# A hybrid decoder layer on one core: half of K in the gate and up projections by seven block products, two of the four weight sums by adding DMAs

## The chip, the cores and the metric

The kernel runs on one core of a Trainium2 chip. The metric is the device time of one execution in microseconds (us); the time given for a kernel is the median of several executions. The engines of the core are PE (matmuls; its weight loads are PEld), DVE and ACT (elementwise work), POOL and SP (here they mainly issue DMAs). Each engine takes its instructions in the order in which the program gives them to it, and waits on semaphores for the others.

## The reference, cut to what matters

One layer over 256 tokens of width 2048, in float32, then a last norm. The mixer (three kinds of attention, gates, output projection) is not touched by the change; the SwiGLU part is.

```python
D_MODEL, SEQ, D_FF = 2048, 256, 5632

def rms_norm(x, g):
    y = x * rsqrt(mean(x * x, axis=-1, keepdims=True) + 1e-6)
    return y * g

def swiglu(h, w_gate, w_up, w_down):
    return (silu(h @ w_gate) * (h @ w_up)) @ w_down

x = x + hybrid_mixer(rms_norm(x, norm_mix_g), ...)
x = x + swiglu(rms_norm(x, norm_ffn_g), w_gate, w_up, w_down)
return rms_norm(x, final_norm_g)
```

## The kernel before, in words

**Matmuls.** All large products go through one scheme. The activations stand transposed (K on the partitions), 128 tokens of them are the loaded operand of a matmul, and 512 columns of a weight are what moves through. To keep float32 accuracy with the faster number format fp32r, each operand is split into a high part (rounded to fp32r) and a low part (the rest), and three products are summed in one PSUM bank: activation high x weight high (L714), high x weight low (L715), low x weight high (L716). In the trace `wh`/`wl` are the parts of a weight, `hq` holds the parts of h, `th`/`tl` those of another transposed operand, `acc` is the bank.

**Pieces.** A weight comes in pieces of 512 rows of K by 512 columns, 1 MB each, loaded by SP (L630) into one of 3 `raw` buffers. A piece is split in two halves of 256 rows: ACT copies the high part (L655) and DVE subtracts it from the raw weights for the low part (L656), 1024 elements per partition each. There are 4 buffers for parts, and `split` runs 3 halves ahead of the products (`AHEAD`). A half feeds 12 matmuls: 2 k-tiles of 128 rows, 2 halves of the tokens (128 each), 3 products.

**Jobs.** A job is one output of 256 tokens by 512 columns: its list of pieces and a closing function. The main loop (L718) goes through the jobs in a fixed order: the mixer's, then four for the output projection (`evac_out`, which makes h, transposed and split, in four quarters of K, keys `("h2", c)`), then for each of 11 blocks j a gate job and an up job, then four of the down projection with 11 pieces each. Per half the loop calls `split` for the half that lies 3 ahead, then `advance(1)`, which lets one step of the waiting side work (a queue of generators, `side`) into the program, then the 12 matmuls.

**Gate and up.** `evac_fg` applies Silu to the two banks of a gate job (ACT, L540); `evac_fu` multiplies with the up banks (DVE, L548) and queues `to_quad`: two groups of four transposes on PE (L203), each followed by the split of 512 elements on ACT (L212) and DVE (L213). The result stays in SBUF until the down jobs read it. A block is 2 jobs x 8 halves x 12 = 192 matmuls.

## Time and profile before

| | |
|---|---|
| time, median of 3 runs | 1689.5 us (1688.86 to 1689.72) |
| the profiled execution: its time / its span | 1689.31 us / 1687.6 us |
| mean granted clock of PE | 0.999 |
| busy: PE, DVE, ACT, POOL | 1675.3, 928.4, 757.0, 28.4 us |
| matmul and transpose instructions on PE | 7644 |
| HBM traffic | 188 GB/s over the span |

The span is the time from the first to the last instruction in the trace; the execution's own time has a little more around it. Busy time is summed per engine; PE's weight loads overlap its matmuls. The granted clock is the share of TensorE's full clock that the chip allowed, 1.00 being 2.4 GHz.

### The profile page before, as it was taken

The numbers are of one execution on the slowest core, as the hardware profiler recorded it, in microseconds if no ns is written. First come the engines' busy times: TensorE is split into PE (matmuls) and PEld (weight loads), VectorE is DVE, ScalarE is ACT, GpSimd is POOL, SyncE is SP. The second block draws the span as 40 slices with busy tenths as digits, with TensorE's granted clock in tenths as the row PEclk, the third lists the DMA queues.
The fourth block names the chain that finished last, engine by engine and source line by source line (L and its number), as shares of the span: only waits on it lengthen the run. The fifth ranks groups of instructions, "written<-read, shape, count | busy, mean of one in ns | idle before, by whom it ended". The sixth has DMA issues, their size and how long they took to land.

```text
span 1687.6 us, 19009 instructions
## 1 busy us (share of the span) xinstructions
PE 1675.3 (99%) x7644; PEld 1380.5 (82%) x7644; DVE 928.4 (55%) x1074; ACT 757.0 (45%) x943; POOL 28.4 (2%) x43
## 2 busy tenths in 40 slices
PE   9999999999999999999999999999999999999997
PEld 6878788888888888888888888888888888888886
DVE  6676765656565656555565555444454445554454
ACT  6354544445444444444445544444444444444443
POOL 2100000000000000000000000000000000000000
PEclk9999999999999999999999999999999999999999
DMA  8545455455555655655655555555555556555553
GB/s 282 188 157 175 150 175 175 157 176 179 181 186 197 204 196 191 206 204 197 222 190 184 178 197 185 189 198 179 197 188 186 197 180 221 182 193 198 197 186 116
DMA packets 47321, 318.06 MB, mean 188 GB/s; under 512 B 5552, under 2 KB 5824, under 8 KB 10240
## 3 DMA queue, kind: packets, MB, share of 16 engines
q1 hardware_dynamic: 44640, 309.35, 52.7%
q0 software_dynamic: 1872, 6.43, 1.5%
q8 instruction: 60, 0.98, 0.2%
q10 hardware_dynamic: 720, 1.06, 0.2%
q14 instruction: 29, 0.24, 0.0%
HBM read 314.72 MB, written 2.10 MB: 188 GB/s over the span
## 4 chain that ended last, share of the span: by engine, by line
PE 99%; DMA 1%; ACT 0%; DVE 0%; SPq 0%; issue 0%; ACTq 0%
PE acc L714 32%; PE acc L716 31%; PE acc L715 31%; PE tps L203 2%; PE sps L242 1%; DMA raw<-w_in_t 1%; PE sps L255 0%; PE sps L256 0%; PE sps L254 0%; PE sps L293 0%; PE sps L294 0%; PE sps L295 0%; SPq L177 0%; ACT x L605 0%; SPq L628 0%; DVE wl L656 0%
## 5 line engine op out<-in xcount | busy, mean ns | idle before, releaser
L656 DVE TENSOR_TENSOR wl<-raw,wh 128x1024 fp32r<-128x1024 f32 x580 | 713.1, 1231 | 714.9 <-ACT wh L655 714.7
L655 ACT ACTIVATE wh<-raw 128x1024 fp32r<-128x1024 f32 x580 | 614.4, 1060 | 820.8 <-PE acc L716 798.1
L714 PE MATMUL acc<-wh,hq 128*128 128x512 f32 x1664 | 663.5, 399 | 0.1
L715 PE MATMUL acc<-wl,hq 128*128 128x512 f32 x1664 | 648.1, 390 | 1.7 <-DVE wl L653 1.0
L716 PE MATMUL acc<-wh,hq 128*128 128x512 f32 x1664 | 649.5, 390 | 0.0
L716 PEld LDWEIGHTS acc<-wh,hq 128*128 128x128 f32 x1664 | 312.3, 188 | 67.4
L715 PEld LDWEIGHTS acc<-wl,hq 128*128 128x128 f32 x1664 | 313.1, 188 | 65.0 <-DVE wl L653 2.2
L714 PEld LDWEIGHTS acc<-wh,hq 128*128 128x128 f32 x1664 | 312.7, 188 | 64.5 <-issue 2.7
L714 PE MATMUL acc<-wh,th 128*128 128x512 f32 x472 | 184.6, 391 | 0.0
L716 PE MATMUL acc<-wh,tl 128*128 128x512 f32 x472 | 183.8, 389 | 0.0
L715 PE MATMUL acc<-wl,th 128*128 128x512 f32 x472 | 183.6, 389 | 0.0
L716 PEld LDWEIGHTS acc<-wh,tl 128*128 128x128 f32 x472 | 88.6, 188 | 18.5
L715 PEld LDWEIGHTS acc<-wl,th 128*128 128x128 f32 x472 | 88.6, 188 | 18.1
L714 PEld LDWEIGHTS acc<-wh,th 128*128 128x128 f32 x472 | 88.6, 188 | 18.2
L714 PE MATMUL acc<-wh,oh 128*128 128x512 f32 x192 | 74.7, 389 | 0.0
L715 PE MATMUL acc<-wl,oh 128*128 128x512 f32 x192 | 74.7, 389 | 0.0
L716 PE MATMUL acc<-wh,ol 128*128 128x512 f32 x192 | 74.7, 389 | 0.0
L716 PEld LDWEIGHTS acc<-wh,ol 128*128 128x128 f32 x192 | 36.0, 188 | 7.5
L715 PEld LDWEIGHTS acc<-wl,oh 128*128 128x128 f32 x192 | 36.0, 188 | 7.5
L714 PEld LDWEIGHTS acc<-wh,oh 128*128 128x128 f32 x192 | 36.0, 188 | 7.5
L266 ACT ACTIVATE sc<-sc,mx 128x128 f32<-128x128 f32 (+1 forms) x32 | 14.3, 448 | 20.2 <-DVE mx L264 19.3
L213 DVE TENSOR_TENSOR tl<-tps,th 128x512 fp32r<-128x512 f32 x30 | 20.5, 684 | 0.0
(161 smaller groups left out, 602.9 us busy)
## 6 DMA issues: line engine op xcount, KB each, us to landing
raw<-w_in_t SPq DMA_DIRECT2D x116, 1024.0 KB, 4.8
raw<-w_fg_t SPq DMA_DIRECT2D x44, 1024.0 KB, 4.8
raw<-w_fu_t SPq DMA_DIRECT2D x44, 1024.0 KB, 4.9
raw<-w_fd_t SPq DMA_DIRECT2D x44, 1024.0 KB, 4.8
raw<-w_branch_t SPq DMA_DIRECT2D x24, 1024.0 KB, 4.8
raw<-w_out_t SPq DMA_DIRECT2D x16, 1024.0 KB, 4.8
raw<-w_in_t SPq DMA_DIRECT2D x7, 512.0 KB, 8.7
bias<-b_gate_r POOLq DMA_DIRECT2D x12, 256.0 KB, 4.2
```

Source lines behind the costliest of these rows:

```text
L203: nc.tensor.transpose(dst[:, i * P:(i + 1) * P], s, ident)
L213: nc.vector.tensor_tensor(l, ps, h.bitcast(F32), OP.subtract)
L242: nc.tensor.matmul(ps[:, a:b], qt[lo:hi, h, t * P:(t + 1) * P], kt[lo:hi, h, 0:b - a], start=True, stop=True)
L266: nc.scalar.activation(sc[:, a:b], sc[:, a:b], AF.Exp, bias=mx[:, t:t + 1], accum_out=sums[:, t:t + 1])
L655: nc.scalar.activation(h, r, AF.Copy)
L656: nc.vector.tensor_tensor(l, r, h.bitcast(F32), OP.subtract)
L714: nc.tensor.matmul(acc, a, wh[:, i], start=pi == 0 and k == 0, stop=False)
L715: nc.tensor.matmul(acc, a, wl[:, i], start=False, stop=False)
L716: nc.tensor.matmul(acc, b, wh[:, i], start=False, stop=pi == npieces - 1 and k == 3)
```

## The change

Only the gate and up projections, their result's way to the down projection, and the pools of buffers change.

The K of 2048 is cut in four quarters of 512. For quarters 0 and 1 the product of the 256 tokens (two halves t of 128) with the up and gate columns of block j is taken as a product of 2 x 2 blocks: A(t, k) times B(k, n), n = 0 for up and n = 1 for gate; B11, B12, B21, B22 are up and gate of quarter 0, up and gate of quarter 1, each a piece of 512 x 512. Instead of eight block products, seven are made (Strassen's scheme in Winograd's form), from sums on both sides. Quarters 2 and 3 are computed as before, two token halves by two columns each.

- The left operands (four sums of A's blocks, and the seven splits) are made once by `combine`, in the steps after the second job of the output projection.
- The four sums of weights are made for each block: B11 += B12 and later B11 += B22 by DVE, in place in the raw buffer; B12 += B22 and the last B11 += B21 by a DMA on POOL's queue that adds the piece from HBM into the raw buffer (`accum_op`).
- `ffn_job` lays out 11 units per block, numbered 0 to 10 in the order of its last lines: an `m_unit` is one block product of 12 matmuls on a single bank, a `p_unit` a plain piece of 24 matmuls on two banks. A unit's `prep` makes sums and splits the whole piece (`whole`, 2048 elements per partition, in place of two halves), its `emit` the matmuls, and then `after`, if it has one.
- There are four banks, b1, b5, b6, b8. `keep` copies a bank to SBUF on ACT when it must be used for another sum: m1 (behind unit 0), m5 (behind unit 2), u2 (behind unit 4), u3 (behind unit 6). Behind u3 the gate's Silu is taken; `last`, behind unit 10, closes the up columns with three DVE operations.
- Parts and raw pieces now share one pool of 12 buffers (`big`): in this stage 6 raw pieces and 3 split units. `prepare_units` calls `prep` of unit u+2 ahead of unit u's matmuls, as many as there are buffers.
- The result f of a block is transposed, copied on ACT and written to DRAM (`f_out`); the first job of the down projection loads it back (`f_load`) and splits it (`f_split`).

A block has 7 x 12 + 4 x 24 = 180 matmuls. The core of the diff:

```diff
 NEG = -1e37
 
-RAW_BUFS = 3
-SPLIT_BUFS = 4
-AHEAD = 3
-SLOTS = 27
+BIGS = 12
+SLOTS = 25
+RAWS = {"mix": 3, "ffn": 6, "down": 3}
+PARTS = {"mix": 4, "ffn": 6, "down": 4}
 LAST = 6
...
+    ht = {}
+
+    def combine(key, h1, h2):
+
+
+        a = {(t, q): h[:, :, t * P:(t + 1) * P] for t in range(2) for q, h in enumerate((h1, h2))}
+        t12 = slot([P, 2, 4, P], "s12")
+        t34 = slot([P, 2, 4, P], "s34")
+        s1, s2, s3, s4 = t12[:, 0], t12[:, 1], t34[:, 0], t34[:, 1]
+        nc.vector.tensor_tensor(s1, a[1, 0], a[1, 1], OP.subtract)
+        nc.vector.tensor_tensor(s2, s1, a[0, 0], OP.subtract)
+        nc.vector.tensor_tensor(s3, a[0, 0], a[1, 0], OP.subtract)
+        nc.vector.tensor_tensor(s4, a[0, 1], s2, OP.add)
+        yield
+        ops = []
+        for v in (a[0, 0], a[0, 1], s4, a[1, 1], s1, s2, s3):
+            p = slot([P, 2, 4, P], "sp", F32R)
+            nc.scalar.activation(p[:, 0], v, AF.Copy)
+            nc.vector.tensor_tensor(p[:, 1], v, p[:, 0].bitcast(F32), OP.subtract)
+            ops.append((p[:, 0], p[:, 1]))
+            yield
+        quads[key] = ops
+        yield
+
...
+                if c < 2:
+                    ht[c] = slot([P, 4, S], "ht")
+                else:
...
+                        if c < 2:
+                            nc.scalar.activation(ht[c][:, k], pk, AF.Copy, scale=gk)
+                            continue
...
+                if c == 1:
+                    yield from combine(("s", 0), ht[0], ht[1])
...
-        job([(w_fu[j, kp], ("h2", kp)) for kp in range(4)], evac_fu(j))
+    f_t = [scratch.tile([P, 4, S], F32, name=f"f_t{j}") for j in range(NCF)]
+
+    def f_out(j, f):
+
+        yield
+        ft = slot([P, 4, S], "ft")
+        for t in range(2):
+            ps = tps()
+            transposes(ps, [f[:, t, i * P:(i + 1) * P] for i in range(4)])
+            nc.scalar.activation(ft[:, :, t * P:(t + 1) * P], ps.rearrange("p (a b) -> p a b", a=4), AF.Copy)
+            if t == 1:
+                nc.gpsimd.dma_start(f_t[j], ft)
+            yield
+
+    f_in = {}
+
+    def f_load(q):
+        if q < NCF:
+            f_in[q] = slot([P, 4, S], "fin")
+            nc.gpsimd.dma_start(f_in[q], f_t[q])
+
+    def f_split(q):
+        h, l = new_both() if q < 4 else new_quad("f")
+        src = f_in.pop(q)
+        nc.scalar.activation(h, src, AF.Copy)
+        nc.vector.tensor_tensor(l, src, h.bitcast(F32), OP.subtract)
+        quads["f", q] = (h, l)
+
+    def ffn_job(j):
+
+
+
+
+
+        B = {(k, n): (j, k, n) for k in range(4) for n in range(2)}
+        B11, B12, B21, B22 = B[0, 0], B[0, 1], B[1, 0], B[1, 1]
+        aps = {(j, k, n): (w_fu, w_fg)[n][j, k] for k in range(4) for n in range(2)}
+        for key in (B22, B11, B12, B[2, 1], B[3, 1], B21, B[2, 0], B[3, 0]):
+            want(key, aps[key], "ffn")
+        bank = {}
+        v = {}
+
+        def add(dst, src):
+            nc.vector.tensor_tensor(raw[dst], raw[dst], raw[src], OP.add)
+
+        def m_unit(op, key, name, adds=(), drop=(), after=None, then=None):
+            def prep():
+                for d, s in adds:
+                    add(d, s)
+                w = whole(raw[key])
+                if then:
+                    nc.gpsimd.dma_start(raw[then[0]], aps[then[1]], accum_op=OP.add)
+                release(*drop)
+                return w
+
+            def emit(w):
+                first = name not in bank
+                if first:
+                    bank[name] = accp.tile([P, 512], F32, tag="acc", name="acc")
+                sh, sl = quad(("s", 0))[op]
+                three(bank[name], sh, sl, w, first, True, True)
+                if after:
+                    after()
+            units.append((2, "ffn", prep, emit))
+
+        def p_unit(k, n, after=None):
+            def prep():
+                w = whole(raw[B[k, n]])
+                release(B[k, n])
+                return w
+
+            def emit(w):
+                qh, ql = quad(("h2", k))
+                for t, name in enumerate((("b1", "b6"), ("b5", "b8"))[n]):
+                    first = name not in bank
+                    if first:
+                        bank[name] = accp.tile([P, 512], F32, tag="acc", name="acc")
+                    three(bank[name], qh[:, :, t * P:(t + 1) * P], ql[:, :, t * P:(t + 1) * P], w, first, True,
+                          True)
+                if after:
+                    after()
+            units.append((2, "ffn", prep, emit))
+
+        def keep(name, b):
+            def f():
+                if name == "m1":
+                    v["m"] = slot([P, 2, 512], "m")
+                    v["u"] = slot([P, 2, 512], "u")
+                v[name] = v["m" if name[0] == "m" else "u"][:, int(name in ("m5", "u3"))]
+                nc.scalar.activation(v[name], bank[b], AF.Copy)
+                if name == "u2":
+                    nc.vector.tensor_tensor(v["m5"], v["m5"], v["u2"], OP.subtract)
+                if name == "u3":
+                    quad("rs2")
+                    s = v["s"] = slot([P, 2, 512], "sg")
+                    nc.vector.tensor_tensor(s[:, 0], bank["b5"], v["m5"], OP.add)
+                    nc.vector.tensor_tensor(s[:, 1], bank["b8"], v["u3"], OP.subtract)
+                    for t in range(2):
+                        nc.scalar.activation(s[:, t], s[:, t], AF.Silu, scale=rs2[:, t:t + 1])
+            return f
+
+        def last():
+
+            s = v["s"]
+            nc.vector.tensor_tensor(s[:, 1], bank["b6"], s[:, 1], OP.mult)
+            nc.vector.tensor_tensor(v["m1"], bank["b1"], v["m1"], OP.add)
+            nc.vector.tensor_tensor(s[:, 0], v["m1"], s[:, 0], OP.mult)
+            side.append(f_out(j, s))
+
+        m_unit(2, B22, "b5")
+        m_unit(0, B11, "b6", after=keep("m1", "b6"))
+        m_unit(4, B11, "b8", adds=[(B11, B12)], after=keep("m5", "b8"), then=(B12, B22))
+        p_unit(2, 1)
+        m_unit(5, B11, "b6", adds=[(B11, B22)], drop=[B22], after=keep("u2", "b6"), then=(B11, B21))
+        p_unit(3, 1)
+        m_unit(6, B12, "b6", drop=[B12], after=keep("u3", "b6"))
+        m_unit(1, B21, "b1", drop=[B21])
+        p_unit(2, 0, after=(lambda: (f_load(0), f_load(1))) if j == NCF - 1 else None)
+        m_unit(3, B11, "b6", drop=[B11])
+        p_unit(3, 0, after=last)
...
+    def release(*keys):
+        for k in keys:
+            del raw[k]
+        pump()
+
+    def three(acc, ah, al, w, start, stop, again=False):
+
+        wh, wl = w
+        n = wh.shape[1]
+        skip = again and not start
+        for k in range(n):
+            nc.tensor.matmul(acc, ah[:, k], wh[:, k], start=start and k == 0, stop=False, skip_group_check=skip)
+            nc.tensor.matmul(acc, ah[:, k], wl[:, k], start=False, stop=False, skip_group_check=skip)
+            nc.tensor.matmul(acc, al[:, k], wh[:, k], start=False, stop=stop and k == n - 1,
+                             skip_group_check=skip)
+
+    def whole(r):
+        h = big([P, 4, 512], "wh", F32R)
+        l = big([P, 4, 512], "wl", F32R)
+        nc.scalar.activation(h, r, AF.Copy)
+        nc.vector.tensor_tensor(l, r, h.bitcast(F32), OP.subtract)
+        return h, l
...
+    pump()
+    ready = deque()
+    held = 0
+    at = 0
+
+    def prepare_units(n):
+
+        nonlocal at, held
+        while at < len(units) and at < n:
+            need, stage, prep, _ = units[at]
+            if held + need > PARTS[stage]:
+                break
+            ready.append(prep())
+            held += need
+            at += 1
+
+    prepare_units(3)
...
+    for u, (need, stage, _, emit) in enumerate(units):
+        prepare_units(u + 4 if stage == "mix" else len(units))
+        advance(1)
+        emit(ready.popleft())
+        held -= need
```

The first place that matters is DVE's order around the beginning of a block (tile numbers are those of the program). Before, at the seam from block 3 to block 4 (the others read alike), DVE had splits (L656), the two multiplications of `evac_fu` (L548) and the splits of the transposed result (L213):

```order
L656 TENSOR_TENSOR wl_8247<-raw_8164,wh_8246 128x1024
L548 TENSOR_TENSOR sg_8121<-acc0_8124,sg_8121 128x512
L548 TENSOR_TENSOR sg_8121<-acc1_8125,sg_8121 128x512
L656 TENSOR_TENSOR wl_8267<-raw_8164,wh_8266 128x1024
L656 TENSOR_TENSOR wl_8285<-raw_8198,wh_8284 128x1024
L213 TENSOR_TENSOR tl_8289<-tps_8290,th_8288 128x4x128
L656 TENSOR_TENSOR wl_8310<-raw_8198,wh_8309 128x1024
L213 TENSOR_TENSOR tl_8289<-tps_8315,th_8288 128x4x128
```

After the change DVE has at the beginning of block 6 the low part of unit 1 (L784, wl_8418), the three operations of `last` (L670 to L672), the sum B11 += B12 (L609), the low parts of units 2 and 3, the sum B11 += B22, and the low part of unit 4:

```order
L784 TENSOR_TENSOR wl_8418<-raw_8282,wh_8417 128x2048
L670 TENSOR_TENSOR sg_8347<-acc_8203,sg_8347 128x512
L671 TENSOR_TENSOR m_8216<-acc_8358,m_8216 128x512
L672 TENSOR_TENSOR sg_8347<-m_8216,sg_8347 128x512
L609 TENSOR_TENSOR raw_8282<-raw_8282,raw_8302 128x2048
L784 TENSOR_TENSOR wl_8450<-raw_8282,wh_8449 128x2048
L784 TENSOR_TENSOR wl_8468<-raw_8332,wh_8467 128x2048
L609 TENSOR_TENSOR raw_8282<-raw_8282,raw_8252 128x2048
L784 TENSOR_TENSOR wl_8498<-raw_8282,wh_8497 128x2048
```

The sums now stand in the queue ahead of the low parts that read them, and the first one behind the closing operations of the block before.

On ACT the same place had, before, high parts of halves (L655) with the high parts of the transposed result (L212) between them:

```order
L655 ACTIVATE wh_8246<-raw_8164 128x1024
L655 ACTIVATE wh_8266<-raw_8164 128x1024
L655 ACTIVATE wh_8284<-raw_8198 128x1024
L212 ACTIVATE th_8288<-tps_8290 128x4x128
L655 ACTIVATE wh_8309<-raw_8198 128x1024
L212 ACTIVATE th_8288<-tps_8315 128x4x128
L655 ACTIVATE wh_8334<-raw_8232 128x1024
```

After the change ACT has the high parts of units 2 (wh_8449) and 3 (wh_8467), the first copy of the old block's transposes (L575), the copy of bank b6 as m1 (L655, acc_8480), the high part of unit 4 (wh_8497), the second copy of the transposes, and the copy of bank b8 as m5 (acc_8511):

```order
L783 ACTIVATE wh_8449<-raw_8282 128x2048
L783 ACTIVATE wh_8467<-raw_8332 128x2048
L575 ACTIVATE ft_8473<-tps_8474 128x4x128
L655 ACTIVATE m_8493<-acc_8480 128x512
L783 ACTIVATE wh_8497<-raw_8282 128x2048
L575 ACTIVATE ft_8473<-tps_8504 128x4x128
L655 ACTIVATE m_8493<-acc_8511 128x512
L783 ACTIVATE wh_8525<-raw_8356 128x2048
```

The copy that frees b8 for unit 3's second half thus stands behind the split of unit 4.

## Rows read from the trace of the kernel before

**Rows 1.** The page: span, busy totals, and the chain that ended last by engine.

```profile
span 1687.6 us, 19009 instructions
...
PE 1675.3 (99%) x7644; PEld 1380.5 (82%) x7644; DVE 928.4 (55%) x1074; ACT 757.0 (45%) x943; POOL 28.4 (2%) x43
...
PE 99%; DMA 1%; ACT 0%; DVE 0%; SPq 0%; issue 0%; ACTq 0%
```

**Rows 2.** Busy time (us) in a stretch of the gate/up stage.

```profile
core 0: us, PE busy (x) PEld busy (x) DVE busy (x) ACT busy (x) POOL busy (x), PEclk, DMA share, GB/s
993.00:1037.50 44.50, 44.50 (x202) 36.85 (x201) 22.04 (x22) 19.21 (x20) 0.00 (x0) 1.00 0.55 189
```

**Rows 3.** Timeline of PE: start, duration, engine, line, operation, tiles, shape, count.

```profile
992.63 0.39 PE L714 MATMUL acc<-wh,hq 128*128 128x512 f32 x1
...
995.35 0.39 PE L714 MATMUL acc<-wh,hq 128*128 128x512 f32 x1
995.58 0.39 PE L715 MATMUL acc<-wl,hq 128*128 128x512 f32 x1
...
996.04 0.60 PE L203 MATMUL tps<-ident,sg 128*128 128x128 f32 x4
...
996.70 0.40 PE L715 MATMUL acc<-wl,hq 128*128 128x512 f32 x1
```

**Rows 4.** Chain that ended last (start, us, what): two neighbouring blocks' transposes.

```profile
1396.46 0.44 PE tps L203 x4
...
1440.93 0.44 PE tps L203 x4
```

**Rows 5.** Timeline of ACT and DVE; in brackets the idle time before and its releaser.

```profile
1396.49 1.06 ACT L655 ACTIVATE wh<-raw 128x1024 fp32r<-128x1024 f32 x1 [1.66 <-PE acc L716]
...
1397.46 0.58 ACT L212 ACTIVATE th<-tps 128x512 fp32r<-128x512 f32 x1
1397.59 1.23 DVE L656 TENSOR_TENSOR wl<-raw,wh 128x1024 fp32r<-128x1024 f32 x1 [1.50 <-ACT wh L655]
```

**Rows 6.** Timeline, a matmul and the split that it releases.

```profile
899.98 0.39 PE L716 MATMUL acc<-wh,tl 128*128 128x512 f32 x1
...
900.41 1.06 ACT L655 ACTIVATE wh<-raw 128x1024 fp32r<-128x1024 f32 x1 [1.60 <-PE acc L716]
```

**Rows 7.** Groups of instructions by line and shape: count, busy us, mean ns.

```profile
L655 ACT ACTIVATE wh<-raw 128x1024 fp32r<-128x1024 f32 x580 | 614.4, 1060 | 820.8 <-PE acc L716 798.1 <-issue 12.5 <-ACT sig L434 7.7
...
L212 ACT ACTIVATE th<-tps 128x512 fp32r<-128x512 f32 x30 | 17.4, 581 | 0.0
...
L540 ACT ACTIVATE sg<-acc,rs 128x512 f32<-128x512 f32 x22 | 15.1, 690 | 9.7 <-PE acc L716 9.7
L548 DVE TENSOR_TENSOR sg<-acc,sg 128x512 f32<-128x512 f32 x22 | 14.1, 682 | 0.0
...
L458 DVE TENSOR_TENSOR sig<-sig,sig 128x1024 f32<-128x1024 f32 x8 | 9.8, 1225 | 0.3
...
L401 ACT ACTIVATE k<-acc 128x512 f32<-128x512 f32 x12 | 7.2, 599 | 7.4 <-PE acc L716 7.4
...
L582 DVE TENSOR_TENSOR x<-x,gfin 128x512 f32<-128x512 f32 x6 | 4.0, 690 | 0.3
...
L652 ACT ACTIVATE wh<-raw 128x512 fp32r<-128x512 f32 x4 | 2.4, 627 | 3.4 <-DMA raw<-w_in_t 3.4
```

**Rows 8.** DMA issues: queue, count, KB of each, median us to landing.

```profile
raw<-w_fg_t SPq DMA_DIRECT2D x44, 1024.0 KB, 4.8
...
gfin<-gfin_r POOLq DMA_DIRECT2D x1, 1024.0 KB, 5.0
```

**Rows 9.** Busy time by stretch, the end of the span (columns as in rows 2).

```profile
1678.00:1679.00 1.00, 0.52 (x3) 0.09 (x1) 0.44 (x2) 0.00 (x0) 0.00 (x0) 1.00 0.00 0
1681.00:1682.00 1.00, 0.00 (x0) 0.00 (x0) 0.86 (x5) 0.20 (x1) 0.00 (x0) 1.00 0.00 0
...
1683.00:1684.00 1.00, 0.00 (x0) 0.00 (x0) 0.00 (x0) 0.67 (x1) 0.00 (x0) 0.50 0.84 313
```

More of the change, by code (lines that the diff above doesn't have):

```diff
@@ L67, in slot, with big @@
         return slots.tile(shape, dt, tag="slot", name=name)
+    def big(shape, name, dt=F32):
+        return bigs.tile(shape, dt, tag="big", name=name)
     def sm(shape, name):
@@ L165, in new_both @@
     def new_both():
[L167 to L168 removed]
+        t = big([P, 2, 4, S], "hq", F32R)
+        return t[:, 0], t[:, 1]
     xq = {}
@@ L552, in trunk @@
-    for j in range(NCF):
-        job([(w_fg[j, kp], ("h2", kp)) for kp in range(4)], evac_fg(j))
-        job([(w_fu[j, kp], ("h2", kp)) for kp in range(4)], evac_fu(j))
+    f_t = [scratch.tile([P, 4, S], F32, name=f"f_t{j}") for j in range(NCF)]
[9 more added lines that the diff above has]
+            yield
@@ L632, in trunk @@
[L632 to L660 removed]
+    units = []
@@ new lines, in trunk, with want, pump @@
+    wanted = []
+    raw = {}
+    loaded = [0]
+    def want(key, ap, stage):
+        wanted.append((key, ap, stage))
+    def pump():
+        while loaded[0] < len(wanted) and len(raw) < RAWS[wanted[loaded[0]][2]]:
+            key, ap, _ = wanted[loaded[0]]
+            n = loaded[0]
+            t = raw[key] = big([P, 4, 512], "raw")
+            if n < 4:
+                for a, w in ((0, 1), (1, 1), (2, 2)) if n == 0 else ((0, 2), (2, 2)):
+                    load_xT(4 * n + a, w)
+                    nc.sync.dma_start(t[:, a:a + w], ap[:, a:a + w])
+            else:
+                nc.sync.dma_start(t, ap)
+            loaded[0] += 1
@@ new lines, in whole, with half @@
+    def whole(r):
[4 more added lines that the diff above has]
+        return h, l
+    def half(r, fine):
+        both = big([P, 2, 2, 512], "wboth", F32R)
+        h, l = both[:, 0], both[:, 1]
+        for sl in (slice(0, 1), slice(1, 2)) if fine else (slice(0, 2),):
+            if fine == 1:
+                split_x(sl.start)
+            nc.scalar.activation(h[:, sl], r[:, sl], AF.Copy)
+            nc.vector.tensor_tensor(l[:, sl], r[:, sl], h[:, sl].bitcast(F32), OP.subtract)
+        return h, l
@@ new lines, in plain_job, with unit, prep, emit @@
+    def plain_job(ji, stage, pieces, evac, before=None, lastjob=False):
+        acc = []
+        late = []
+        def unit(pi, hf):
+            key = (ji, pi)
+            def prep():
+                if ji == 0 and (pi or hf):
+                    for i in range(2):
+                        split_x(4 * pi + 2 * hf + i)
+                if stage == "down" and ji == down0 and hf == 0:
+                    f_load(pi + 2)
+                    f_split(pi)
+                w = half(raw[key][:, 2 * hf:2 * hf + 2], (1 + hf) if ji == 0 and pi == 0 else 0)
+                if hf:
+                    release(key)
+                return w
+            def emit(w):
+                first = pi == 0 and hf == 0
+                final = pi == len(pieces) - 1 and hf == 1
+                if first:
+                    if before:
+                        before()
+                    acc.extend(accp.tile([P, 512], F32, tag="acc", name=f"acc{t}") for t in range(2))
+                def part(t, w=w):
+                    qh, ql = quad(pieces[pi][1])
+                    k = slice(2 * hf, 2 * hf + 2)
+                    three(acc[t], qh[:, k, t * P:(t + 1) * P], ql[:, k, t * P:(t + 1) * P], w, first, final)
+                part(0)
+                if lastjob and 2 * (len(pieces) - pi) - hf <= LAST:
+                    late.append(part)
+                else:
+                    part(1)
+                if final:
+                    if lastjob:
+                        finish(0, acc[0])
+                        for p in late:
+                            p(1)
+                        finish(1, acc[1])
+                    else:
+                        evac(acc)
+            units.append((1, stage, prep, emit))
+        for pi, (ap, _) in enumerate(pieces):
+            want((ji, pi), ap, stage)
+            for hf in range(2):
+                unit(pi, hf)
@@ new lines, in trunk @@
+    for ji, (ps, evac) in enumerate(jobs):
+        before = None
+        if ji in starts:
+            before = lambda a=starts[ji]: load_bias(*a)
+        elif ji >= out_job:
+            before = lambda c=ji - out_job: load_x(c)
+        plain_job(ji, "mix", ps, evac, before)
+    for j in range(NCF):
+        ffn_job(j)
+    down0 = len(jobs)
+    for c in range(4):
+        plain_job(down0 + c, "down", [(w_fd[c, kp], ("f", kp)) for kp in range(NCF)],
+                  evac_down(c), None if c else load_gfin, c == 3)
```

122 lines of the change are left out of this document (7 added, 115 removed).

## The prediction

> **What bounds the kernel now.** The first view is the page's busy totals with the chain that ended last: PE is busy 1675.3 of 1687.6 us and is 99% of the chain [rows 1]. The reader is to see that no other engine, queue or DMA stands on it. Next comes busy time by stretch: of a 44.50 us window in the gate/up stage PE takes all 44.50, DVE 22.04, ACT 19.21 [rows 2]. Then the timeline gives PE's prices [rows 3]. Two matmuls twelve apart start at 992.63 and 995.35: 2.72 us for twelve, 0.2267 each. Three matmuls with four transposes among them take 995.58 to 996.70, 1.12 us where three alone take 0.68: 0.44 for four transposes. A block j (gate and up of 512 columns) is 192 matmuls and two groups of transposes, 43.53 + 0.88 = 44.41 us; the chain shows the same transposes of two neighbouring blocks 44.47 apart [rows 4]. So PE does nothing but its own work, and only the other engines' order can spoil that. Their timeline is read last [rows 5]: before each split ACT waits 1.66 us for a matmul to free a buffer, DVE then 1.50 for ACT. A split is released at 900.41, 0.20 after the slot in which the next matmul could start (899.98 + 0.2267) [rows 6]. An operation whose inputs are ready starts 0.09 before the one ahead of it ends (1397.46 against 1396.49 + 1.06), and one that waits for the other engine starts 0.04 after.
>
> **What the change removes.** Per block the seven products take 84 matmuls where eight take 96: 180 x 0.2267 + 0.88 = 41.69 us. That is 2.72 less, 29.9 over 11 blocks. The seven left operands are made once, without a matmul. If PE never waits, the time is 1689.3 - 29.9 = 1659.4, from the profiled execution's own time.
>
> **Prices that no row shows.** The parts of a whole piece are now one operation of 2,048 elements per partition. On DVE 512 elements take 690 ns and 1,024 take 1,225, so 535 per 512 more and 2.295 us for 2,048; on ACT 627 and 1,060 give 1.93 [rows 7]. The ends: two operations of 1,024, 2.45 and 2.12; or the slope alone with no fixed part, 4 x 535 = 2.14 and 4 x 433 = 1.73. I take the line, since both points lie on it. The sum B11 + B12 has the same size on DVE: 2.295. Per block DVE then has 11 low parts, 2 sums and 6 short operations, 33.9 us, and ACT 11 splits, four copies of 0.60, two Silu of 0.69 and two copies of 0.58, 26.2 us. Neither fills 41.7 us; what decides is where they stand.
>
> **The walk through one block.** Time 0 is when PE ends unit 10 of the block before; units are numbered as in the list of ffn_job. Unit u+2 is prepared when unit u starts, into buffers that unit u-1 frees.
>
> First place, unit 2. DVE's order is: the three closing operations of the old block, the sum for unit 2, its low part. The closing operations wait for unit 10's last matmul (0.20) and take 0.68 + 0.60 + 0.73 (the third waits for the second): 2.21. The sum runs 2.13 to 4.42. ACT's split of unit 2 reads the sum, 4.46 to 6.39, and the low part follows, 6.43 to 8.73. PE has units 0 and 1 and two groups of transposes until then: 5.44 + 0.88 = 6.32. Its first matmul of unit 2 needs the high part alone, the second the low part; that would start at 6.55 and starts at 8.77. PE waits **2.22 us**. Unit 2 ends at 11.26.
>
> Second place, the middle of unit 3. It adds one half to bank b5, the other to b8, and b8 must first be copied out as m5. On ACT that copy stands behind the split of unit 4, which waits for the second sum. DVE does unit 3's low part 8.64 to 10.94, then that sum to 13.15; ACT's split runs 13.19 to 15.12, the copy of the old block's transposes to 15.61, the copy of b8 from 15.53 to 16.13. PE wants b8 at 11.26 + 2.72 = 13.98 and gets it at 16.17: **2.19 us**. So what queues behind one sum on DVE is a split, and behind that split on ACT is a copy for which PE waits.
>
> After that the queues catch up. Unit 4's low part is ready at 17.46 (wanted at 18.9), unit 5's at 20.3 (21.6), unit 6's at 23.4 (27.0), and the later units have longer cover. The block takes 41.69 + 2.22 + 2.19 = 46.10, 1.69 more than 44.41, and eleven make +18.6. The first block has the residual additions of the last output column in place of the closing operations, two of 0.68, and transposes and splits of its own; I count it as the others. With the low prices the two waits are 1.71 and 1.68, +7.3 in all; with the high ones 2.72, 2.69 and 0.37 at unit 9, +33.6.
>
> **Adding DMAs.** POOL issues the first once DVE's sum has read the target (4.42); ACT needs it for unit 6 at about 19.1: 14.7 us. The second leaves after unit 4's low part (17.46), for unit 9 at about 33.5: 16 us. A plain 1 MB transfer that POOL issued took 5.0 us, one from SP 4.8 [rows 8]. No row has an adding one. The near bound is 5.0; the far bound is three such transfers one behind another, 15, for a read, a read and a write that do not overlap. I take a price under 14.7, thus nothing. The Trainium skill, page "Collectives: The Full Stack", section "The bandwidth ceiling: the fold count and why AG ≠ RS ≠ AR", says that a sum made in the DMA engines reads two sources for each chunk and runs at about half the rate of a copy. By it the transfer would take an estimated 10 us, and the sum stays as it is; no row here shows it.
>
> **Costed at nothing.** The left operands are 11 DVE and 7 ACT operations of 512 elements (7.6 and 4.2 us), spread over nine units in the output projection; a unit there is 2.72 us with 1.23 of DVE and 1.06 of ACT in splits. Uncovered they would cost those 7.6 once. Plain loads keep four units or more of lead, over 10 us against 4.8. The round trip of f through DRAM has whole blocks of cover going out and four units of 2.72 coming back, against 5.0. Its splits in the first job of down (1.06 and 1.23 per two units) fit in 5.44. The mixing stage keeps its three halves of lead.
>
> **Sum.** 1689.3 + 18.6 = 1707.9, and 0.2 up to the median of the runs, 1689.5: **1708**.
>
> **Rivals.**
> *PE never waits: 1659.4, the other side.* No engine is full, and busy sums say PE still leads by 7.8 us a block. Its place is unit 2: the chain there (closing operations, sum, split, low part) must shrink from 8.73 to 6.51. For it: the averages. Against it: each link waits for the one ahead and their prices come from rows. Break-even needs the two waits down to 2.72 together, about 2.0 us on DVE and 1.70 on ACT for 2,048 elements, below the slope. Chance 0.13, with the part just around break-even.
> *An adding DMA comes late.* If it takes over 16.4 us, each microsecond more is one more per block: 18 us gives 1708 + 1.6 x 11 = 1726, 22 gives 1770. For it: two reads and a write while plain loads hold the DMA engines at 0.55 [rows 2]. Against it: over three times the plain price is allowed. Chance 0.13; the page's rule on two reads brings it nearer without reaching it.
> *The clock falls in the waits.* Rows show the granted clock at 1.00 in 1681 to 1682, when the last matmul had ended at 1678.5, and at 0.50 (1.2 GHz) in 1683 to 1684 [rows 9]. A wait of 2.2 us is shorter than those 2.5 us at full clock, but there are two within 10 us, in each block. If each set the next twelve matmuls to half speed, that is 2.72 a wait, 5.4 a block, 60 in all: 1768. The Trainium skill, page "TensorE: Matmul & The Clock Gate", section "HAM oscillation — how this bites in real kernels", says that a wait repeated in each tile can bring the lower clock back each time; the end of this trace agrees that idling lowers it, and no row shows waits of this length repeated. Chance 0.06.
>
> **How the numbers follow.** The forecast, two waits a block, has 0.68, and lies between 1697 and 1723 by the price bounds. The range must reach into the cases beside it: 1690 leaves the waitless case out, and 1735 takes in an adding DMA of up to 18.8 us. I stretch the lower end to 1682 for a second wait that is smaller than walked. That holds 0.8. Faster, by over 0.2% (about what a measurement of this kernel can tell from no change), has 0.11 from the first rival; within it 0.03, its break-even part and the forecast's lowest edge; slower 0.86.
>
> **What would show it.** Right: 1,980 matmuls in the stage at 0.2267 us; a block of about 46.1 us; in each block DVE idle for unit 2's split, PE idle about 2.2 us for a low part and again for the copy of b8; the granted clock at 1.00; whole splits of about 1.93 and 2.3 us. Wrong: a block of 41.7 us without those waits; ACT waiting for POOL's transfers at units 6 or 9; a clock under 1.00 behind a wait; or new waits in the mixing or down stages, which I take as untouched.

## The result

The changed kernel takes 1718.7 us (median of 4 runs, 1715.0 to 1721.4) against 1689.3: a ratio of 1.0173, 95% interval 1.0153 to 1.0192 (intervals below are 95% too). It is slower, as forecast, by 29.4 us where 18.6 were forecast. The page of the changed kernel (profiled execution 1718.48 us) answers to [rows 1]:

```profile
span 1716.6 us, 18675 instructions
...
PE 1667.7 (97%) x7512; PEld 1365.3 (80%) x7512; DVE 1069.0 (62%) x1077; ACT 829.4 (48%) x950; POOL 58.7 (3%) x87
```

PE is idle 48.9 us of the span where it was idle 12.3 before. The next view sums what PE waited for (engine, tile and line that waited, what for: us in total, times, longest):

```profile
PE acc L776 <- DVE wl L784: 19.5, 11, 1.8
...
PE acc L775 <- ACT m L655: 15.9, 11, 5.0
```

Both waits are those of the forecast, once in each of 11 blocks: a low part of DVE (unit 2) and the copy of b8 as m5 on ACT (the middle of unit 3). No wait of PE or of a split in this stage is for a DMA. (The page's chain names an adding DMA once, ahead of ACT's copy at 1434.88 in block 10; that copy starts as the split ahead of it ends, and in the program it waits for PE alone.) The prices that no row of before had are these (groups by line and shape: count, busy us, mean ns; then the idle time before them and its releasers):

```profile
L784 DVE TENSOR_TENSOR wl<-raw,wh 128x2048 fp32r<-128x2048 f32 x121 | 276.2, 2292 | 131.9 <-ACT wh L783 128.1 <-PE acc L777 1.3 <-PE acc L776 0.5
L783 ACT ACTIVATE wh<-raw 128x2048 fp32r<-128x2048 f32 x121 | 229.2, 1912 | 195.6 <-DVE raw L609 129.9 <-PE acc L776 32.2 <-issue 30.3
...
L609 DVE TENSOR_TENSOR raw<-raw 128x2048 f32<-128x2048 f32 x22 | 50.3, 2285 | 0.0
```

2,292 ns on DVE and 1,912 on ACT stand against 2,295 and 1,930 taken from the line through two points of [rows 7]; the sum costs 2,285.

**One block, followed.** In block 2 the first matmul of unit 0 starts at 1046.19. DVE's timeline (start, duration, engine, line, operation, tiles, shape, count; in brackets the idle time before it and its releaser):

```profile
1046.39 0.69 DVE L670 TENSOR_TENSOR sg<-acc,sg 128x512 f32<-128x512 f32 x1 [1.42 <-PE acc L777]
...
1048.32 2.29 DVE L609 TENSOR_TENSOR raw<-raw 128x2048 f32<-128x2048 f32 x1
1052.67 4.50 DVE L784 TENSOR_TENSOR wl<-raw,wh 128x2048 fp32r<-128x2048 f32 x2 [2.06 <-ACT wh L783]
1057.08 2.29 DVE L609 TENSOR_TENSOR raw<-raw 128x2048 f32<-128x2048 f32 x1
1061.40 2.29 DVE L784 TENSOR_TENSOR wl<-raw,wh 128x2048 fp32r<-128x2048 f32 x1 [2.04 <-ACT wh L783]
```

ACT's timeline of the same place:

```profile
1050.72 3.71 ACT L783 ACTIVATE wh<-raw 128x2048 fp32r<-128x2048 f32 x2 [8.08 <-DVE raw L609]
...
1059.46 1.91 ACT L783 ACTIVATE wh<-raw 128x2048 fp32r<-128x2048 f32 x1 [4.05 <-DVE raw L609]
1061.28 0.58 ACT L575 ACTIVATE ft<-tps 128x512 f32<-128x512 f32 x1
1061.75 0.59 ACT L655 ACTIVATE m<-acc 128x512 f32<-128x512 f32 x1
```

And the two matmuls of PE that waited:

```profile
1055.01 0.50 PE L776 MATMUL acc<-wl,sp 128*128 128x512 f32 x1 [1.83 <-DVE wl L784]
...
1062.39 0.50 PE L775 MATMUL acc<-wh,h2h 128*128 128x512 f32 x1 [1.86 <-ACT m L655]
```

The reader is to see the forecast's chain link by link. The sum starts 2.13 us into the block (forecast 2.13), the split of unit 2 at 4.53 (4.46), the low part at 6.48 (6.43), the matmul that waited for it at 8.82 (8.77). The second sum starts at 10.89 (10.94 less 0.09), the split of unit 4 at 13.27 (13.19), the copy of the old transposes behind it, the copy of b8 at 15.56 (15.53), the matmul at 16.20 (16.17). DVE is idle 2.06 and 2.04 us behind the two sums, since the split on ACT has to read each sum before DVE's next low part can follow.

**The blocks' lengths** come from PE's timeline, as the time from one block's first matmul to the next one's; a wait is what a gap between two matmuls has over 0.2267, transposes taken off.

| kernel | block 0 | blocks 1 to 10 | time, us |
|---|---|---|---|
| kernel before | 45.0 | 44.5 | 1689.3 |
| changed kernel | 51.7 | 46.3 in eight, 47.9 and 48.1 | 1718.7 |
| b8's copy first | 47.5 | 44.7 in seven, 45.7 in three | 1697.4 |
| sum early | 49.2 | 42.9 to 43.0 | 1678.3 |
| both edits | 44.9 | 41.75 | 1662.8 |
| no adding DMA | 50.9 | 46.3 to 46.5 in six, 47.9 in four | 1718.3 |
| eight products | 46.2 | 44.5 | 1690.7 |
| four DVE sums | 50.4 | 44.4, the last 44.7 | 1692.5 |
| no sums | 43.0 | 41.75 | 1659.8 |
| block 0's steps alone | 47.9 | 46.3 in seven, 47.9, 47.9 and 48.2 | 1717.4 |
| both edits and block 0's steps | 42.2 | 41.75 | 1660.0 |

**The clock.** In block 1 PE resumes at 1008.75 behind its first wait. Busy time by stretch (columns as in [rows 2]; the granted clock is third from the end):

```profile
1009.00:1010.00 1.00, 1.00 (x5) 0.80 (x5) 1.00 (x1) 0.14 (x1) 0.00 (x0) 1.00 0.90 188
1010.00:1011.00 1.00, 1.00 (x4) 0.80 (x3) 1.00 (x2) 0.00 (x0) 0.00 (x0) 0.56 1.00 262
...
1012.00:1013.00 1.00, 1.00 (x4) 0.78 (x3) 1.00 (x1) 0.00 (x0) 0.00 (x0) 0.50 0.95 262
1013.00:1014.00 1.00, 1.00 (x5) 0.83 (x4) 0.10 (x1) 0.81 (x1) 0.00 (x0) 0.73 1.05 426
1014.00:1015.00 1.00, 1.00 (x6) 0.82 (x5) 0.00 (x0) 1.00 (x1) 0.00 (x0) 1.00 1.08 344
```

Some 1.4 us after PE resumed, the granted clock falls to 0.50 (1.2 GHz) and is back at 1.00 within four microseconds. The second wait of this block is then 0.4 us in place of 2.0: what the clock took, the wait gave back, since ACT and DVE went on meanwhile and b8 was wanted later. The block is 46.24 us, and block 2, at 1.00 throughout, is 46.30. In block 8 the fall comes behind the second wait (PE resumes at 1340.00):

```profile
1340.00:1341.00 1.00, 1.00 (x4) 0.86 (x5) 1.00 (x1) 1.00 (x1) 0.00 (x0) 1.00 1.06 451
1341.00:1342.00 1.00, 1.00 (x4) 0.80 (x3) 0.52 (x2) 0.75 (x1) 0.16 (x1) 0.61 0.05 16
...
1343.00:1344.00 1.00, 1.00 (x4) 0.81 (x3) 1.00 (x1) 0.00 (x0) 0.27 (x1) 0.50 0.83 82
```

Nothing behind it takes the loss up, and the block is 47.85. In this trace the fall lies between the waits in blocks 1, 3, 5, 7 and 10 and behind both in 8 and 9; blocks 2, 4 and 6 have none.

**Block 0** is 51.7 us. Here the last quarter of h is still being made. ACT's timeline:

```profile
960.96 1.91 ACT L783 ACTIVATE wh<-raw 128x2048 fp32r<-128x2048 f32 x1 [4.13 <-DVE raw L609]
962.78 0.46 ACT L541 ACTIVATE h2h<-tps,gf 128x256 fp32r<-128x256 f32 x1
965.63 0.47 ACT L541 ACTIVATE h2h<-tps,gf 128x256 fp32r<-128x256 f32 x1 [2.39 <-DVE h2l L542]
966.00 0.59 ACT L655 ACTIVATE m<-acc 128x512 f32<-128x512 f32 x1
```

DVE's:

```profile
962.91 2.29 DVE L784 TENSOR_TENSOR wl<-raw,wh 128x2048 fp32r<-128x2048 f32 x1 [2.04 <-ACT wh L783]
965.12 0.48 DVE L542 SCALAR_TENSOR_TENSOR h2l<-tps,gf,h2h 128x256 fp32r<-128x256 f32 x1
```

PE's:

```profile
966.64 0.79 PE L775 MATMUL acc<-wh,h2h 128*128 128x512 f32 x1 [4.98 <-ACT m L655]
```

ACT's second high part of h (965.63) waits for DVE's first low part of h (965.12), because the loop takes one of ACT and one of DVE in turn; that low part stands behind the low part of unit 4 (962.91 to 965.20), and the copy of b8 (966.00) behind the high part. PE waits 5.1 us in place of 2.0. Before this wait ends the granted clock has fallen to 0.50, and it stays there until 972.6 (columns as in [rows 2]):

```profile
967.00:972.00 5.00, 5.00 (x13) 3.83 (x13) 3.04 (x3) 2.49 (x4) 0.00 (x0) 0.50 1.02 182
```

The matmuls behind the wait thus lose another 2.9 us, of which 0.1 is PE taking up its pace. The wait at unit 2 is shorter here, 1.5 in place of 2.1.

The adding DMAs (queue, count, KB of each, median us to landing), as in [rows 8]:

```profile
raw<-w_fg_t SPq DMA_DIRECT2D x44, 1024.0 KB, 8.2
...
raw<-w_fg_t POOLq DMA_DIRECT2D x11, 1024.0 KB, 9.5
raw<-w_fu_t POOLq DMA_DIRECT2D x11, 1024.0 KB, 9.3
```

They take 9.3 to 9.5 us, and the plain loads of the stage 7.7 to 8.2 where they took 4.8. Both stay inside their cover, 14.7 us and over 10. The way of f through DRAM took 12.5 us out and 9.6 back, where the prediction reckoned with 5.0; PE waited for neither.

### The profile page after: what moved, and what is told of

It reads as the page before. It is cut to its first block, busy times and chain, and to the rows that moved or that the text cites. A ratio compares the mean times of both kernels' runs of the same rounds, so it can differ in the third digit from the quotient of the medians.

```text
span 1716.6 us, 18675 instructions
## 1 busy us (share of the span) xinstructions
PE 1667.7 (97%) x7512; PEld 1365.3 (80%) x7512; DVE 1069.0 (62%) x1077; ACT 829.4 (48%) x950; POOL 58.7 (3%) x87
## 5 line engine op out<-in xcount | busy, mean ns | idle before, releaser
L794 DVE TENSOR_TENSOR wboth<-raw,wboth 128x1024 fp32r<-128x1024 f32 (+1 forms) x410 | 499.7, 1230 | 298.5 <-ACT wboth L793 298.1
L793 ACT ACTIVATE wboth<-raw 128x1024 fp32r<-128x1024 f32 (+1 forms) x410 | 427.0, 1053 | 406.3 <-PE acc L777 307.7
L775 PE MATMUL acc<-wboth,hq 128*128 128x512 f32 x1088 | 437.3, 402 | 1.1 <-ACT wboth L793 1.1
L777 PE MATMUL acc<-wboth,hq 128*128 128x512 f32 x1088 | 425.1, 391 | 0.0
L776 PE MATMUL acc<-wboth,hq 128*128 128x512 f32 x1088 | 423.9, 390 | 1.2 <-DVE wboth L794 1.0
L784 DVE TENSOR_TENSOR wl<-raw,wh 128x2048 fp32r<-128x2048 f32 x121 | 276.2, 2292 | 131.9 <-ACT wh L783 128.1
L783 ACT ACTIVATE wh<-raw 128x2048 fp32r<-128x2048 f32 x121 | 229.2, 1912 | 195.6 <-DVE raw L609 129.9
L777 PEld LDWEIGHTS acc<-wboth,hq 128*128 128x128 f32 x1088 | 204.2, 188 | 44.6
L775 PEld LDWEIGHTS acc<-wboth,hq 128*128 128x128 f32 x1088 | 204.6, 188 | 43.8 <-issue 2.7
L776 PEld LDWEIGHTS acc<-wboth,hq 128*128 128x128 f32 x1088 | 204.7, 188 | 42.5 <-DVE wboth L794 2.5
L775 PE MATMUL acc<-wh,h2h 128*128 128x512 f32 x352 | 141.2, 401 | 15.9 <-ACT m L655 15.9
L776 PE MATMUL acc<-wl,h2h 128*128 128x512 f32 x352 | 139.8, 397 | 0.0
L775 PE MATMUL acc<-wh,sp 128*128 128x512 f32 x308 | 125.2, 406 | 0.0
L777 PE MATMUL acc<-wh,sp 128*128 128x512 f32 x308 | 123.1, 400 | 0.0
L776 PE MATMUL acc<-wboth,fh 128*128 128x512 f32 x224 | 87.2, 389 | 0.0
L775 PE MATMUL acc<-wboth,fh 128*128 128x512 f32 x224 | 87.1, 389 | 0.0
```

The lines of the kernel that those rows point to most:

```text
L775: nc.tensor.matmul(acc, ah[:, k], wh[:, k], start=start and k == 0, stop=False, skip_group_check=skip)
L776: nc.tensor.matmul(acc, ah[:, k], wl[:, k], start=False, stop=False, skip_group_check=skip)
L777: nc.tensor.matmul(acc, al[:, k], wh[:, k], start=False, stop=stop and k == n - 1, skip_group_check=skip)
L783: nc.scalar.activation(h, r, AF.Copy)
L784: nc.vector.tensor_tensor(l, r, h.bitcast(F32), OP.subtract)
L793: nc.scalar.activation(h[:, sl], r[:, sl], AF.Copy)
```

## The experiments

Two theories at first. **Order:** both waits come from what stands ahead in DVE's and ACT's queues; moving two instructions removes them, and the clock's falls go with them. **DMA:** the 22 adding DMAs slow the loads, hold the raw buffers, and so make splits late.

**1. The copy of b8 first.** ACT copies b8 before it splits unit 4; the second sum stays where it was on DVE.

```diff
...
-                w = whole(raw[key])
-                if then:
-                    nc.gpsimd.dma_start(raw[then[0]], aps[then[1]], accum_op=OP.add)
-                release(*drop)
-                return w
+                box = []
+
+                def rest():
+                    box.append(whole(raw[key]))
+                    if then:
+                        nc.gpsimd.dma_start(raw[then[0]], aps[then[1]], accum_op=OP.add)
+                    release(*drop)
+                if hold:
+                    v["rest"] = rest
+                else:
+                    rest()
+                return box
...
                 nc.scalar.activation(v[name], bank[b], AF.Copy)
+                if name == "m5":
+                    v["rest"]()
...
-        m_unit(5, B11, "b6", adds=[(B11, B22)], drop=[B22], after=keep("u2", "b6"), then=(B11, B21))
+        m_unit(5, B11, "b6", adds=[(B11, B22)], drop=[B22], after=keep("u2", "b6"), then=(B11, B21),
+               hold=True)
```

> Edit: the copy of bank b8 as m5 stands on ACT ahead of unit 4's split (the second sum stays where it was on DVE, unit 4's split follows unit 2). Queue order theory: the wait in the middle of unit 3 (2.0 us in blocks where the clock is full, 0.4 where it had just fallen) goes, the wait of 2.1 us at unit 2 stays. If one wait a block no longer lowers the clock, a block falls from 46.3 to 43.9 us and the time from 1718.7 to about 1690; if each wait at unit 2 still costs its 1.9 us of half clock, a block is 45.8 and the time about 1710. Rival, adding DMAs and contention: nothing changes, 1718.

Measured: 1697.4 us (1.0047 of before, 1.0032 to 1.0062), 21 us under the changed kernel. The wait in unit 3 is gone, the one of 2.1 at unit 2 stays, and unit 4's low part is 0.4 late in its turn. Seven blocks have 44.7 us at full clock; in three the clock falls behind the one wait, as in block 6 (PE resumes at 1227.81):

```profile
1226.00:1229.00 3.00, 1.19 (x5) 1.02 (x6) 3.00 (x2) 2.68 (x4) 0.02 (x1) 1.00 0.85 172
1229.00:1232.00 3.00, 3.00 (x8) 2.29 (x8) 3.00 (x2) 0.17 (x1) 0.55 (x1) 0.52 0.97 265
1232.00:1235.00 3.00, 3.00 (x13) 2.43 (x12) 0.89 (x2) 3.00 (x3) 0.00 (x0) 0.91 0.94 345
```

Neither branch of the expectation on the clock holds alone: one wait of 2.1 us lowers it in some blocks and not in others. A fall costs a block 1.0 us here: 1.4 at half clock, less the 0.4 by which unit 4's low part is then no longer late.

**2. The first sum early.** B11 += B12 goes right behind unit 1's low part, ahead of the three closing operations, and the old block's transposes one unit later.

```diff
                 w = whole(raw[key])
+                for d, s in post:
+                    add(d, s)
...
-        m_unit(0, B11, "b6", after=keep("m1", "b6"))
-        m_unit(4, B11, "b8", adds=[(B11, B12)], after=keep("m5", "b8"), then=(B12, B22))
+        m_unit(0, B11, "b6", post=[(B11, B12)], after=keep("m1", "b6"))
+        m_unit(4, B11, "b8", after=keep("m5", "b8"), then=(B12, B22))
...
     def f_out(j, f):
 
         yield
+        yield
```

> Edit: the sum B11 += B12 is made right behind unit 1's low part, ahead of the three closing operations of the old block; the old block's transposes come one unit later. Queue order theory: the wait at unit 2 goes; the second sum moves up too, so that the copy of b8 is late by about 0.5 us. A block of 42.4 us, about 1675. If the clock falls in this stage without such waits, 1.9 us more a block, about 1695. Rival, contention: 1718.

Measured: 1678.3 us (0.9932, 0.9917 to 0.9947). The wait at unit 2 is gone, and the second is 1.1 where 0.5 was expected, which makes the block 42.9. No block but the first has the clock fall. PE's one wait of block 1, and ACT ahead of it:

```profile
1052.75 0.50 PE L778 MATMUL acc<-wh,h2h 128*128 128x512 f32 x1 [0.91 <-ACT m L658]
```

```profile
1049.81 1.92 ACT L786 ACTIVATE wh<-raw 128x2048 fp32r<-128x2048 f32 x1 [3.73 <-DVE raw L610]
1051.63 0.57 ACT L576 ACTIVATE ft<-tps 128x512 f32<-128x512 f32 x1
1052.10 0.59 ACT L658 ACTIVATE m<-acc 128x512 f32<-128x512 f32 x1
```

The copy of b8 (1052.10) stands behind the split of unit 4 and the old transposes' copy, as before, only earlier.

**3. Both edits.** The two diffs together.

> Both edits. Queue order theory: no wait in blocks 1 to 10, clock 1.00, a block of 41.8 us, 1662 to 1670 in all. Rival, the stage is held by loads and adding DMAs (9.4 us each, loads 8 in place of 4.8): waits for DMAs appear, over 1690.

Measured: 1662.8 us (0.9844, 0.9828 to 0.9861), faster than the kernel before by 27 us. Block 2, busy time by stretch (columns as in [rows 2]):

```profile
1034.64:1076.39 41.75, 41.75 (x189) 34.57 (x188) 33.21 (x20) 25.24 (x19) 2.30 (x3) 1.00 0.80 265
```

PE is busy all 41.75 us, with DVE at 33.21 and the DMA engines at 0.80, above the 0.73 of the changed kernel's same block. The DMA theory falls: the plain loads still take 6.7 to 8.5 us, the adding DMAs 8.2 and 12.4, and PE waits for nothing in blocks 1 to 10.

**4. No adding DMA.** Left out: the 22 DMAs with the sums B12 += B22 and the last B11 += B21.

```diff
                 if then:
-                    nc.gpsimd.dma_start(raw[then[0]], aps[then[1]], accum_op=OP.add)
+                    pass
```

> Edit: the 22 adding DMAs are left out, with them the sums B12 += B22 and the last B11 += B21; DVE's sums stay. Queue order theory: within the runs of the changed kernel, 1715 to 1722. Rival, the adding DMAs cost time by contention or by late landing: faster by 10 us or more, plain loads back at 4.9 us.

Measured: 1718.3 us (1.0168, 1.0153 to 1.0183), within the runs of the changed kernel. The plain loads are back at 4.8 and 4.9 us, as the page shows for one of the two weights:

```profile
raw<-w_fg_t SPq DMA_DIRECT2D x44, 1024.0 KB, 4.9
```

The waits are 2.1 and 2.0 as before. Here the clock falls behind both waits in four blocks, where it did in two, so the total alone could hide some 3 us. But a block at full clock is 46.3 us with the adding DMAs and without them: they cost nothing here.

**5. Eight products in the new frame.** All eight pieces as plain units; whole splits, the shared pool and f's way through DRAM stay. The left operands and the copies of banks go with the seven products.

```diff
-        m_unit(2, B22, "b5")
...
-        p_unit(3, 0, after=last)
+        for k in range(4):
+            p_unit(k, 1, after=gate if k == 3 else None)
+        for k in range(4):
+            p_unit(k, 0, after=last if k == 3 else (lambda: (f_load(0), f_load(1))) if k == 2 and j == NCF - 1
+                   else None)
```

> Edit: the seven products are undone alone. All eight pieces of a block are plain units (192 matmuls, no sums, no adding DMA, no copies of banks), while whole splits, the shared pool of buffers, and f's way through DRAM stay. If all that was costed at nothing is hidden, as forecast, a block is 44.4 us and the time that of the kernel before, 1687 to 1692. Rival: the new buffers, whole splits or the round trip of f cost something; then slower by that, with a wait in the trace that names it.

Measured: 1690.7 us against 1689.2 (1.0009, 0.9999 to 1.0018); the operations that close a block stand 44.47 us apart (1037.16 to 1081.63), as in [rows 4]. What stays here of the things costed at nothing costs at most 3 us, by the interval. The trace has 1.2 us more in the stage, all of it in block 0 (46.2 against 45.0), where PE waits 1.0 us for the row factors on DVE.

**6. Four sums on DVE.** Both edits, with DVE sums in place of the adding DMAs.

```diff
-        m_unit(4, B11, "b8", after=keep("m5", "b8"), then=(B12, B22))
+        m_unit(4, B11, "b8", after=keep("m5", "b8"))
...
-        m_unit(5, B11, "b6", adds=[(B11, B22)], drop=[B22], after=keep("u2", "b6"), then=(B11, B21),
+        m_unit(5, B11, "b6", adds=[(B11, B22)], after=keep("u2", "b6"),
...
-        p_unit(3, 1)
+        p_unit(3, 1, post=[(B12, B22)], drop=[B22])
...
-        m_unit(1, B21, "b1", drop=[B21])
+        m_unit(1, B21, "b1", post=[(B11, B21)], drop=[B21])
```

> Edit: the order without waits (both edits of the run before), and the two adding DMAs replaced by DVE sums of 2.29 us, one behind unit 5's low part, one behind unit 7's. DVE then has about 38.5 of 41.75 us a block. If only the places count, no wait: 1661 to 1666, the adding DMAs buy nothing. If DVE's total load counts, low parts come late behind it: 1 us or more a block, over 1675.

Measured: 1692.5 us (1.0018, 1.0009 to 1.0027). This was a miss of the first expectation: the block is 44.4, as long as before the change. Busy time of one block, and the place where PE waits first, on DVE and PE:

```profile
1042.39:1086.79 44.40, 42.65 (x190) 34.25 (x188) 37.36 (x22) 25.12 (x19) 0.56 (x1) 1.00 0.53 201
```

```profile
1065.83 2.29 DVE L799 TENSOR_TENSOR wl<-raw,wh 128x2048 fp32r<-128x2048 f32 x1
1068.04 2.28 DVE L610 TENSOR_TENSOR raw<-raw 128x2048 f32<-128x2048 f32 x1
1070.24 2.28 DVE L799 TENSOR_TENSOR wl<-raw,wh 128x2048 fp32r<-128x2048 f32 x1
...
1076.33 4.49 DVE L799 TENSOR_TENSOR wl<-raw,wh 128x2048 fp32r<-128x2048 f32 x2 [2.61 <-ACT wh L798]
```

```profile
1072.58 0.50 PE L791 MATMUL acc<-wl,h2h 128*128 128x512 f32 x1 [1.38 <-DVE wl L799]
```

DVE is busy 37.4 us of 44.4 and still too late: the low part of unit 8 (1070.24) stands behind a sum (1068.04). DVE's 7.0 idle us are mostly forced: 2.04 behind each of two sums, for a split on ACT, and 2.61 ahead of 1076.33, while ACT does Silu and the next split. So a DVE that is not full can still be late, since its load counts together with the turns that it must wait. Other places for the two sums were not tried; how much is due to the places and how much to the load stays open. Against sums at these places the two adding DMAs buy 30 us (1662.8 against 1692.5).

**7. No sums at all.** The changed kernel's order, without any of the four sums.

> Edit: the changed kernel's order as it is, with all four sums of weights left out (DVE's two and the two DMAs). Queue order theory: with no sum ahead of them the split of unit 2 is released at once and the split of unit 4 no longer holds the copy of b8; no wait in blocks 1 to 10, clock 1.00, a block of 41.8 us, 1661 to 1668. Rival, the closing operations or the copies themselves hold PE: waits of a similar size stay, over 1690.

Measured: 1659.8 us (0.9823, 0.9807 to 0.9840), every block from 1 on 41.75, clock 1.00. The closing operations and the copies hold nothing by themselves. What holds is DVE's two sums in front of the splits, since the adding DMAs alone made no difference (experiment 4).

**8. Block 0's steps.** The changed kernel, with ACT's two high parts of h ahead of DVE's two low parts.

```diff
-                        if c < 2:
-                            nc.scalar.activation(ht[c][:, k], pk, AF.Copy, scale=gk)
-                            continue
-                        nc.scalar.activation(h[:, k], pk, AF.Copy, scale=gk)
+                        nc.scalar.activation((ht[c] if c < 2 else h)[:, k], pk, AF.Copy, scale=gk)
+                    for i in range(2 if c > 1 else 0):
+                        k = 2 * kp + i
+                        gk = gf[:, 4 * c + k:4 * c + k + 1]
+                        pk = ps[:, i * S:(i + 1) * S]
                         nc.vector.scalar_tensor_tensor(l[:, k], pk, gk, h[:, k].bitcast(F32),
```

> Edit: in the steps that make h (the changed kernel's order otherwise), ACT's two high parts of a group of transposes stand ahead of DVE's two low parts, in place of one and one. If block 0's wait of 5.1 us in unit 3 comes from the copy of b8 standing on ACT behind a second high part that waits for DVE's first low part, which stands behind unit 4's low part, that wait falls by about 2.4 us to 2.7; the other blocks stay at 46.3 or 47.9. About 1716, within the runs of the changed kernel by time, so it is read from block 0 in the trace. Rival, the wait has another cause: it stays at 5.1.

Measured: 1717.4 us (1.0167, 1.0150 to 1.0184). ACT and PE in block 0:

```profile
961.22 1.91 ACT L784 ACTIVATE wh<-raw 128x2048 fp32r<-128x2048 f32 x1 [4.13 <-DVE raw L610]
963.04 0.82 ACT L538 ACTIVATE h2h<-tps,gf 128x256 fp32r<-128x256 f32 x2
963.75 0.59 ACT L656 ACTIVATE m<-acc 128x512 f32<-128x512 f32 x1
```

```profile
964.40 0.79 PE L776 MATMUL acc<-wh,h2h 128*128 128x512 f32 x1 [2.47 <-ACT m L656]
```

The high parts stand together, the copy of b8 starts at 963.75, and the wait is 2.6 us; block 0 is 47.9, 3.8 less, of which 1.3 is less time at the lower clock. As expected, the time alone could not have told it.

**9. Both edits, with block 0's steps, and the row factors spread one unit later.** To the diffs of 1, 2 and 8 comes:

```diff
                     row_rstd(rs2, ssq2)
                     yield
                     yield
+                    yield
                     to_row(rsrow, rs2)
```

> Edit: the order without waits (both earlier edits), with the same reordering of h's parts, and the step that spreads the row factors one unit later. Block 0 loses its two waits of 0.9 and 1.4 us, from 44.9 to 42.6 us; the other blocks stay at 41.75. About 1660.5. Rival: the later step meets the Silu that needs it and the wait only moves; 1662.7 as before.

Measured: 1660.0 us (0.9825, 0.9811 to 0.9840). Block 0 is 42.2 and has no wait left. This is the fastest of all, 29 us under the kernel before; its page:

```profile
span 1658.4 us, 18691 instructions
...
PE 1644.5 (99%) x7512; PEld 1355.7 (82%) x7512; DVE 1068.0 (64%) x1077; ACT 831.5 (50%) x950; POOL 59.1 (4%) x87
...
PE 98%; DMA 1%; ACT 0%; DVE 0%; SPq 0%; issue 0%; ACTq 0%
```

PE is 98% of the chain again, with 132 matmuls and transposes fewer than in [rows 1].

## Why the prediction was right, and where it was off

**The sign and its mechanism** held. The walk gave two waits of 2.22 and 2.19 us in a block of 46.10; at full clock they are 2.09 and 2.02 in one of 46.3, with some 0.4 more beside the waits: the first matmul of unit 2 comes 0.2 late, as it starts when the split of its high part ends, and behind each wait PE loses 0.1 in taking up its pace. Experiments 1, 2 and 3 remove them one by one by order alone, 7 by leaving out what the splits wait for.

**What it costed at nothing** held. Experiment 7 has the left operands, the pools and f's way through DRAM, and takes 1659.8 where the sum without waits was 1659.4; experiment 9 has the adding DMAs too and takes 1660.0. The adding DMAs landed between the two bounds, 5.0 and 15. The Trainium skill, page "Collectives: The Full Stack", section "The bandwidth ceiling: the fold count and why AG ≠ RS ≠ AR", states its half rate for the reducing step of a collective, and the prediction made an estimated 10 us of it; the trace, with 9.3 to 9.5, agrees with the number. That a second read is the reason is not shown, since plain loads in the same stage took 7.7 to 8.2. The rival of a late adding DMA (chance 0.13) did not occur. Its 16.4 us stands in the prediction without a working, beside covers of 14.7 and 16; no adding DMA's median reached either (12.4 at most, in experiments 3 and 9).

**The size was off by 10.6 us** of 29.2, in the profiled execution (1718.48 against 1707.9). The gate and up stage took 517.8 us (948.22 to 1466.05) where it took 489.7 (948.36 to 1438.04), 28.15 more, against 18.6 in the forecast, which was 9.6 too low. The step that failed is "the first block ... I count it as the others". It is 6.8 longer than the first block of the kernel before (44.95, other blocks 44.47), 5.1 more than the 1.69 forecast. The named additions ("transposes and splits of its own") were seen and their queue not walked. The wait for the copy of b8 is 2.9 longer than the 2.2 walked, the matmuls behind it lose 2.9 more, nearly all to the lower clock, and the wait at unit 2 is 0.7 shorter. Experiment 8 shows that 3.8 us come from one ACT operation that waits behind one of DVE. Blocks 8 and 9, where the clock falls behind both waits, are 3.7 longer together than forecast, and the other eight 0.8. The last 1.0 lies behind the last matmul (10.5 us from its start to the end of the span in place of 9.5). PE, DVE and ACT do the same there at the same distances, and the last output DMA, issued 5.56 us behind that start in both, landed at 8.86 in place of 8.26; why it did stays open.

**The rival of the clock** (chance 0.06) had half of it right, and "a clock under 1.00 behind a wait" was one of the prediction's own signs of being wrong. The falls come, in block 0 and in seven of the ten others, but it priced each wait at 2.72 us more, 60 in all. They cost at most 3.5 in blocks 8 and 9 (47.85 and 48.1 against 46.26) and some 2.8 in block 0. The five that lie between two waits cost nothing, since they are paid out of the second. The Trainium skill, page "TensorE: Matmul & The Clock Gate", section "HAM oscillation — how this bites in real kernels", says that a wait repeated in each tile can bring the lower clock back each time; the trace agrees in seven blocks of ten, and with the one long wait of experiment 1 (2.1 us) in three.

**The rival on the other side** (PE never waits, 1659.4) did not occur in the changed kernel, but its number was right: with the waits taken out by order it is 1660.0. What it asked for, a chain of 6.51 us in place of 8.73 at unit 2, came from order, not from cheaper operations.

## What to carry to other kernels

An operation that saves the bound engine work can still put links into a chain on two others: count, for each queue, what stands ahead of the instruction for which the bound engine waits, and not the busy share (DVE was at 72% of a block in which it held PE twice). When such a wait is found on paper, look first for an instruction that can move ahead of the slow one: here two moves, with the old block's transposes one unit later, turned 1718.7 into 1662.8. Walk the first and the last round of a loop by themselves, since other work is still in their queues.

## What the runs showed that was not expected

- A fall of the clock can cost nothing: 3 us at 0.50 between two waits shortened the second from 2.0 to 0.4 us.
- In blocks 1 to 10 the clock fell in 7, 8 and 6 of 10 with waits of 2.1 and 2.0 us (changed kernel, experiments 4 and 8), in 3 of 10 with waits of 2.1 and 0.4 (experiment 1), and in none with one of 1.1, or with waits of 1.5 and 0.5 (experiments 2 and 6).
- An adding DMA of 1 MB from HBM into SBUF took 9.3 to 9.5 us in the changed kernel (8.0 to 12.4 in the others) where a plain one took 4.8 to 5.0, and beside them the plain loads took 7.7 to 8.2; without them they were back at 4.8 and 4.9.
